# One DiT layer on one core: another order of the first loads, and an FFN stage with folded columns, gate rows in two passes and features that go by DRAM

## The chip, the cores and the metric

The kernel runs on one core of a Trainium2 chip, and its metric is the device time of one execution in microseconds (us). The core's engines are PE (matmul; its weight loads are shown apart as PEld), DVE (vector), ACT (scalar), POOL (GpSimd) and SP, which here only issues DMAs. Each engine works through its own list in order. DMAs that SP and ACT issue stand in two queues.

## The reference, cut to what is computed

```python
sh1, sc1, g1, sh2, sc2, g2 = split(silu(c) @ w_ada + b_ada, 6)        # ada: 2048 -> 6 x 2048
u  = x * (1 + sc1) + sh1                                              # 256 latent tokens
uc = ctx * (1 + csc1) + csh1                                          # 256 context tokens, their own ada row
q, k, v = u @ w_in, uc @ w_in                                         # 2048 -> 3072; 16 heads of 128, 4 kv heads
heads = [window attention with sinks (8 heads), global attention with normed q, k (8 heads)]
x = layer_norm(ALPHA * x + g1 * (heads @ w_out)) * ln1_g + ln1_b
z = x * (1 + sc2) + sh2
x = layer_norm(ALPHA * x + g2 * ((silu(z @ w_gate) * (z @ w_up)) @ w_down)) * ln2_g + ln2_b   # 2048 -> 5632 -> 2048
```

All inputs and the output are float32.

## The kernel before

**Products.** Every large product is made of three: each operand is split into a high part, rounded to the type f32r (ACT casts it), and a low part, the rest (DVE subtracts it). `mm3` (lines 277 to 280) then issues x_high·w_high, x_high·w_low and x_low·w_high into one PSUM bank, a row tile of 128 tokens against 512 columns. A matmul in plain float32 stands twice in the trace, in f32r once.

**Weights** come in tiles of 1 MB (`load_raw`, L248, on SP's queue) into 4 buffers of the pool `raw`, and are split in two halves (`split_raw`: ACT `hi` L268, DVE `lo` L269) into 4 pairs of buffers `hi`, `lo`. A weight tile is 24 matmuls of the FFN stage: 4 slices of 128 features, 2 row tiles, 3 products.

**First part, up to about 404 us.** A planner (class `Flow`) gets steps with costs, dependences, earliest times (`since`) and buffers, and writes the instructions of all engines in the order that it finds. It holds the ada vector for layer norm 1's inputs, the q/k/v product in five groups of features (`GROUPS`), attention, and the output product. The context and the latent `u` need ada columns: PE multiplies `cs` (silu of c) with w_ada (L570), or DVE does it with weighted sums (`vector_sum`, `csum`, `adav`, `g1b`). `WARM` small matmuls against the identity (L1237) are steps of the planner that keep PE at work where it has nothing; `EARLY_WARM` of them (L322) stand ahead of the first transposition. The planner's list for PE starts with its free time in the table at line 460.

**The start.** ACT issues the DMAs of `c` and `c_ctx` (crow), waits for PE to transpose them, takes silu, and only then issues the first 128 columns of x and ctx and the ada bias `brow` (L333 to L336). PE transposes `brow` at L466 and x at L738.

**FFN stage, first half** (`first_half`, from 404 to about 590 us). Gate and up of the first ten of eleven column blocks f are made in two halves. For f < `ONE_F` the first half takes only the features 0 to 511, else 0 to 1023 (`groups`); the sums go to buffers `spills`. Meanwhile (`merge` interleaves lists evenly) the features 512 to 2047 of z are made ready: DVE sums w_ada rows over 16 steps into `adav`, a row on each partition (`ada_vector_steps`, L393); `second_columns_of` turns them into columns, 8 float32 matmuls against `ones` (L1099), or 4 in `second_scales` (L1395); POOL makes the scale mA and shift mB (`combine`, L1092 to L1094); `z_part` transposes two slices of the normed x on PE (L1434), applies scale and shift on ACT (L1438) and splits (L1440, L1441) into `u2h`, `u2l`, on which the later matmuls work.

```python
    run(merge(first_half[3 : 2 * ONE_F], scales))
    combine(1)
    z_part(4)
    z_part(6)
    cutoff = len(first_half) - 2
    run(merge(first_half[2 * ONE_F : cutoff], side))
    for kk in range(EARLY_G * 4, KD, 2):
        z_part(kk)
    run(first_half[cutoff:])
```

Here `side` is the sums and columns of the feature groups 2 and 3. Outside the planner's part the framework's scheduler sets the order of the instructions on each engine.

**Second half and down product.** The other features follow; hidden features reach their transposed layout by DVE block transposes (`squares`), DMAs to DRAM (`put`, 4 per row tile) and back (`get`), without PE. Beside the down product, DVE sums the rows of the gate g2, and a float32 matmul against `ones` (`rows_from`, L403) spreads each of four pieces of 512 over the partitions.

Of the kernel before, what the change touches and what calls it, by code (L numbers as in the profile page):

```python
# [22 lines left out]
P = 128  # L23
D = 2048
# [24 lines left out]
EARLY_WARM = 2  # L49
COLD = 7  # L50
# [3 lines left out]
ONE_F = 3  # L54
# [149 lines left out]
def dit_layer(ctx: ExitStack, tc: tile.TileContext, x, c, cx, c_ctx, w_ada, b_ada, w_in, q_norm_g,  # L204
# [114 lines left out]
    nc.scalar.dma_start(crow[KD : 2 * KD, :], c_ctx.rearrange("(k p) -> k p", p=P))  # L319
    early = wk_bank()  # L320
# [11 lines left out]
    first_cx = xt[:, :, D - P :]  # L332
    nc.scalar.dma_start(xt[:, :, :P], x[:, :P].rearrange("(t p) d -> p t d", p=P))  # L333
    nc.scalar.dma_start(first_cx, cx[:, :P].rearrange("(t p) d -> p t d", p=P))
    brow = pa.tile([6 * KD, P], F32, tag="brow", name="brow")
    nc.scalar.dma_start(brow, b_ada.rearrange("o (n p) -> (o n) p", p=P))  # L336
# [6 lines left out]
    ones = main.tile([P, P], F32, tag="ones", name="ones")  # L343
    nc.gpsimd.memset(ones, 1.0)
# [54 lines left out]

    def rows_from(sb, dst, s):  # L400
# [36 lines left out]
    def const_tables():  # L437
        nc.gpsimd.tensor_scalar_mul(nsink, sinkb, -1.0)
        for t in range(NT):
            for g, cg, sg in ((gq, cosQ, sinQ), (gk, cosK, sinK)):  # L440
# [19 lines left out]
             {"SP": 1300.0, "PE": 3500.0, "ACT": 5000.0, "DVE": 4000.0, "POOL": 4000.0})  # L460
# [43 lines left out]
    def flow_weights(w, k0, nk, c0, width=NB, where=("raw", "araw"), spare=False):  # L504

        raw, ld = flow_load(w, k0, nk, c0, width, where)
        pieces = []
        for s in range(0, nk * width, SUB * NB):
            n = min(SUB * NB, nk * width - s)
            hl = Buf("b4" if spare else "hl")  # L510
            hl.rooms = [hl, Buf("b4")] if spare else [hl]

            def cast(hl=hl, s=s, n=n):
                if spare:
                    hl.hi, hl.lo = (b4([P, SUB * NB], F32R, c) for c in ("hi", "lo"))
                else:
# [7 lines left out]
            a = F.add("ACT", 60 + 0.87 * n, cast, [ld], hl.rooms)  # L524
# [32 lines left out]
    def flow_columns(c0, ncol, shift, scale, ats, at):  # L557
# [253 lines left out]
    def flow_blocks(g, bs, where=("raw", "araw")):  # L811

        k0, n = GROUPS[g]
        if n == 1:
            for i, (b0, m) in enumerate(((2, 1), (0, 2), (3, 2), (5, 1))):
                F.at = bs[0] + (bs[1] - bs[0]) * i / 4
                piece, = flow_weights(w_in, k0, 1, b0 * NB, m * NB, ("b4",))
# [284 lines left out]

    def second_place(g, ps):
# [288 lines left out]
    def second_scales(sb):  # L1392
        ps = wk_bank()
        for j in range(4):
            nc.tensor.matmul(ps[:, 2 * j : 2 * j + 2], lhsT=sb[:, j * P : (j + 1) * P], rhs=ones[:, 0:2], start=True, stop=True)  # L1395
        nc.vector.tensor_scalar_add(sc2[:, 4:8, :], ps[:, 0:8].rearrange("p (j s) -> p j s", s=2), 1.0)
# [33 lines left out]
    def z_part(kk):  # L1430
        ps = wk_bank()
        for j in range(2):
            for t in range(NT):
                nc.tensor.transpose(ps[:, (j * 2 + t) * P : (j * 2 + t + 1) * P],  # L1434
                                    xt[:, t, (kk + j) * P : (kk + j + 1) * P], ident)
        uf = pb.tile([P, 2, SEQ], F32, tag="t2k", name="uf2", bufs=4)
        for j in range(2):
            nc.scalar.activation(uf[:, j, :], ps[:, j * SEQ : (j + 1) * SEQ], AF.Identity,  # L1438
                                 bias=mB[:, kk + j : kk + j + 1], scale=mA[:, kk + j : kk + j + 1])
        nc.scalar.copy(u2h[:, kk : kk + 2, :], uf)  # L1440
        nc.vector.tensor_tensor(u2l[:, kk : kk + 2, :], uf, u2h[:, kk : kk + 2, :].bitcast(F32), op=ALU.subtract)  # L1441
# [102 lines left out]
    scales = ada_vector_steps((4 * D + NB,), NB, lambda: late_sums[1]()[:, :NB], second_scales)  # L1544
# [25 lines left out]
    scalars(1)  # L1570
    adav1 = vector_sums(NB)
# [160 lines left out]
```

## Time and profile before

| | |
|---|---|
| time, median of 3 runs | 1138.57 us (1138.26 to 1139.23) |
| time of the profiled execution | 1141.69 us, of which its span is 1139.9 |
| PE busy | 1116.1 us, 98% of the span, 5287 instructions |
| DVE, ACT, POOL busy | 859.9 us (75%), 564.2 us (49%), 42.0 us (4%) |
| DMA | 321.26 MB, mean 282 GB/s |
| shares of the chain that ended last | PE 85%, DVE 7%, DMA 5%, issue 1%, ACT 1% |

The span is the profiled stretch of one execution; its time is 1.8 us more, and 3.1 us above the median of the runs. The chain is followed back from the last instruction to whatever released each step. A busy PE is not a PE at its peak, since the ends of matmuls are modelled: how fast it goes is seen in the distance of their starts.

### The profile page before, as it was taken

How to read it: one execution, taken by the hardware profiler on the slowest of the kernel's cores; microseconds unless marked ns; L12 is line 12 of the kernel's file. 1: busy time of each engine (PE TensorE's matmuls, PEld its weight loads, DVE VectorE, ACT ScalarE, POOL GpSimd, SP SyncE). 2: the span in 40 equal slices, each digit the busy share in tenths (PEclk: the TensorE clock that was granted, in tenths of full speed). 3: DMA queues.
4: the chain of work that ended last, by engine and by line, in shares of the span. 5: the costliest groups of instructions: out<-in, count | busy, mean ns of one | idle time of the engine just before them, and what ended most of it. 6: DMA issues, size and time to landing. Idle time of an engine off the chain costs nothing.

```text
span 1139.9 us, 14170 instructions
## 1 busy us (share of the span) xinstructions
PE 1116.1 (98%) x5287; PEld 903.9 (79%) x5287; DVE 859.9 (75%) x1074; ACT 564.2 (49%) x815; POOL 42.0 (4%) x82
## 2 busy tenths in 40 slices
PE   7999999999999999999999999999999999999995
PEld 6766778787888788888888888888888888888884
DVE  3758999999998897767767566776766787676556
ACT  2435574877785265444464444445444344333441
POOL 1000040101200000010000000000000000000000
PEclk9999999999999999999999999999999999999998
DMA  9999999788999689989866776777676989877531
GB/s 299 353 363 394 399 338 371 250 277 251 340 333 398 230 315 324 320 310 316 304 217 222 236 238 223 231 246 257 218 251 238 314 314 332 317 273 264 193 134 74
DMA packets 186413, 321.26 MB, mean 282 GB/s; under 512 B 8764, under 2 KB 51164, under 8 KB 184039
## 3 DMA queue, kind: packets, MB, share of 16 engines
q1 hardware_dynamic: 184536, 319.25, 80.7%
q10 hardware_dynamic: 1808, 1.11, 0.3%
q8 instruction: 41, 0.67, 0.2%
q14 instruction: 28, 0.23, 0.1%
HBM read 304.07 MB, written 16.25 MB: 281 GB/s over the span
## 4 chain that ended last, share of the span: by engine, by line
PE 85%; DVE 7%; DMA 5%; issue 1%; ACT 1%; SPq 0%; DVEq 0%; ACTq 0%
PE acc L278 26%; PE acc L280 25%; PE acc L279 25%; DMA raw<-in_w_ada_dram 3%; PE wk L1046 2%; DVE csum L634 2%; DMA raw<-in_w_in_dram 2%; DVE g1b L393 2%; PE wk L570 1%; DVE lo L522 1%; DMA brow<-in_b_ada_dram 1%; PE wk L278 1%; PE wk L280 1%; PE wk L279 1%; PE wk L403 1%
## 5 line engine op out<-in xcount | busy, mean ns | idle before, releaser
L269 DVE TENSOR_TENSOR lo<-raw,hi 128x1024 fp32r<-128x1024 f32 x258 | 312.5, 1221 | 179.7 <-ACT hi L268 176.3
L268 ACT CAST hi<-raw 128x1024 fp32r<-128x1024 f32 x258 | 271.0, 1055 | 343.8 <-PE acc L280 296.8
L278 PE MATMUL acc<-hi,u2h 128*128 128x512 f32 x704 | 274.6, 390 | 0.0
L280 PE MATMUL acc<-hi,u2l 128*128 128x512 f32 x704 | 274.1, 389 | 0.0
L279 PE MATMUL acc<-lo,u2h 128*128 128x512 f32 x704 | 274.0, 389 | 0.0
L280 PEld LDWEIGHTS acc<-hi,u2l 128*128 128x128 f32 x704 | 132.1, 188 | 27.9 <-DVE u2l L1556 0.5
L278 PEld LDWEIGHTS acc<-hi,u2h 128*128 128x128 f32 x704 | 132.2, 188 | 27.9 <-ACT u2h L1555 0.8
L279 PEld LDWEIGHTS acc<-lo,u2h 128*128 128x128 f32 x704 | 132.2, 188 | 27.8 <-DVE lo L269 0.4
L278 PE MATMUL acc<-hi,hTh 128*128 128x512 f32 x344 | 135.5, 394 | 0.0
L280 PE MATMUL acc<-hi,hTl 128*128 128x512 f32 x344 | 133.9, 389 | 0.0
L279 PE MATMUL acc<-lo,hTh 128*128 128x512 f32 x344 | 133.9, 389 | 0.0
L519 ACT CAST hi<-raw 128x1024 fp32r<-128x1024 f32 (+1 forms) x86 | 87.7, 1032 | 93.0 <-PE acc L280 54.0
L393 DVE SCALAR_TENSOR_TENSOR adav<-raw,cs,adav 128x512 f32<-128x512 f32 (+1 forms) x128 | 121.2, 947 | 12.6 <-DMA raw<-in_w_ada_dram 10.9
L522 DVE TENSOR_TENSOR lo<-raw,hi 128x1024 fp32r<-128x1024 f32 (+1 forms) x86 | 101.7, 1196 | 22.7 <-ACT hi L519 22.6
L278 PE MATMUL acc<-hi,uh 128*128 128x512 f32 x256 | 103.4, 404 | 0.8 <-ACT acc L534 0.8
L279 PE MATMUL acc<-lo,uh 128*128 128x512 f32 x256 | 100.3, 392 | 1.5 <-DVE lo L522 1.5
L280 PE MATMUL acc<-hi,ul 128*128 128x512 f32 x256 | 100.1, 391 | 0.1
L278 PEld LDWEIGHTS acc<-hi,hTh 128*128 128x128 f32 x344 | 64.6, 188 | 14.4 <-issue 1.0
L279 PEld LDWEIGHTS acc<-lo,hTh 128*128 128x128 f32 x344 | 64.6, 188 | 14.3 <-issue 1.0
L280 PEld LDWEIGHTS acc<-hi,hTl 128*128 128x128 f32 x344 | 64.6, 188 | 13.3
L278 PEld LDWEIGHTS acc<-hi,uh 128*128 128x128 f32 x256 | 48.2, 188 | 17.7 <-issue 5.0
L279 PEld LDWEIGHTS acc<-lo,uh 128*128 128x128 f32 x256 | 48.2, 188 | 11.5 <-DVE lo L522 2.6
(216 smaller groups left out, 1195.7 us busy)
## 6 DMA issues: line engine op xcount, KB each, us to landing
raw<-in_w_ada_dram SPq DMA_DIRECT2D x63, 1024.0 KB, 7.5
raw<-in_w_gate_dram SPq DMA_DIRECT2D x44, 1024.0 KB, 6.2
raw<-in_w_up_dram SPq DMA_DIRECT2D x44, 1024.0 KB, 5.3
raw<-in_w_down_dram SPq DMA_DIRECT2D x44, 1024.0 KB, 5.0
raw<-in_w_ada_dram SPq DMA_DIRECT2D x66, 512.0 KB, 6.4
raw<-in_w_in_dram SPq DMA_DIRECT2D x18, 1024.0 KB, 7.9
raw<-in_w_out_dram SPq DMA_DIRECT2D x16, 1024.0 KB
pd<-hx SPq DMA_DIRECT2D x64, 128.0 KB, 3.9
```

What stands on the lines that cost most here:

```text
L268: nc.scalar.copy(hi[:, :n], raw[:, s : s + n])
L269: nc.vector.tensor_tensor(lo[:, :n], raw[:, s : s + n], hi[:, :n].bitcast(F32), op=ALU.subtract)
L278: nc.tensor.matmul(ps, lhsT=xh, rhs=w[0], start=first, stop=False, skip_group_check=seeded)
L279: nc.tensor.matmul(ps, lhsT=xh, rhs=w[1], start=False, stop=False, skip_group_check=seeded)
L280: nc.tensor.matmul(ps, lhsT=xl, rhs=w[0], start=False, stop=last, skip_group_check=seeded)
L393: nc.vector.scalar_tensor_tensor(a[:, c : c + piece], raw[:, f : f + piece], cs[:, 4 * (g * (G4 * NB // w) + j) + 2, None], a[:, c : c + p ...
L403: nc.tensor.matmul(ps, lhsT=ones, rhs=sb[:, s : s + NB], start=True, stop=True)
L519: nc.scalar.copy(hl.hi[:, :n], raw.t[:, s : s + n])
L522: nc.vector.tensor_tensor(hl.lo[:, :n], raw.t[:, s : s + n], hl.hi[:, :n].bitcast(F32), op=ALU.subtract)
L570: nc.tensor.matmul(bank.t[32 * j : 32 * j + 32, :width], lhsT=cs[:, 4 * k + 2 - 2 * i : 4 * k + 34 - 2 * i], rhs=raw.t[:, c * width : (c + ...
L634: nc.vector.scalar_tensor_tensor(a, src, cs[:, k, None], a, op0=ALU.mult, op1=ALU.add)
L1046: nc.tensor.matmul(o_ps.t[:, : 2 * P].rearrange("p (g q) -> p g q", q=32), lhsT=v, rhs=pv[:, k], start=k == 0, stop=k == 3)
```

## The change

1. **Start.** ACT issues `brow`, x and ctx right behind `c` and `c_ctx`, ahead of its wait for PE. `EARLY_WARM` goes from 2 to 5; of the 56 planned warm-ups 3 in place of 7 are costed as cold; PE's list starts at 5600 in place of 3500; three `since` times are set. With other times the planner finds another order for the whole first part.
2. **Columns.** `columns_by_squares` replaces the float32 matmuls against `ones` for the groups 1 to 3: per 512 columns a DVE block transpose and a DVE sum over 32, then the 4 small matmuls of `fold_parts`, which the first part has already (L685).
3. **Normed features.** The 24 PE transposes of `z_part` go. DVE makes block transposes of the normed x into unused `spills` (`z_squares`), SP's queue carries them to DRAM (`z_puts`) and back (`z_gets`) into the place of `u2h`, and `z_place` applies scale and shift from there. Puts and gets are steps merged into the FFN stage, the puts behind 2 empty steps.
4. **Gate rows.** Each piece is split in two f32r parts (ACT, DVE), and two f32r matmuls replace the float32 one.
5. `ONE_F` 3 to 4: block f = 3 takes only the features 0 to 511 in the first half. `ones` is written by ACT, no longer by POOL.

```diff
-EARLY_WARM = 2
-COLD = 7
+EARLY_WARM = 5
+COLD = 3
...
-ONE_F = 3
+ONE_F = 4
...
+    brow = pa.tile([6 * KD, P], F32, tag="brow", name="brow")
+    nc.scalar.dma_start(brow, b_ada.rearrange("o (n p) -> (o n) p", p=P))
+    first_cx = xt[:, :, D - P :]
+    nc.scalar.dma_start(xt[:, :, :P], x[:, :P].rearrange("(t p) d -> p t d", p=P))
+    nc.scalar.dma_start(first_cx, cx[:, :P].rearrange("(t p) d -> p t d", p=P))
     early = wk_bank()
...
+    def add_rows(ps, pair):
+        nc.tensor.matmul(ps, lhsT=ones_r, rhs=pair[0], start=True, stop=False)
+        nc.tensor.matmul(ps, lhsT=ones_r, rhs=pair[1], start=False, stop=True)
...
-                rows_from(sb, dst, s)()
+                pair = [pb.tile([P, NB], F32R, tag="t2k", name="rowpair", bufs=4) for _ in range(2)]
+                split_rows(pair, sb[:, s : s + NB])
+                ps = wk_bank()
+                add_rows(ps, pair)
+                nc.scalar.copy(dst[:, s : s + NB], ps)
...
+    def columns_by_squares(sb, n):
+
+        ps = wk_bank()
+        part = pb.tile([P, 1, n * 4], F32, tag="part", name="part", bufs=2)
+        for s in range(0, n * P, NB):
+            turned = pb.tile([P, NB], F32, tag="t2k", name="turned", bufs=4)
+            nc.vector.transpose(turned, sb[:, s : s + NB])
+            nc.vector.reduce_sum(part[:, 0, s // 32 : (s + NB) // 32], turned.rearrange("p (b j) -> p b j", j=32), axis=AX.X)
+        fold_parts(ps, part, n)
+        return ps[:, :n, None]
...
-            second_place(g, second_columns_of(sb))
+            place_columns(g, columns_by_squares(sb, 8))
             combine(g)
...
+    def z_squares(n, t):
+        squares(xt[:, t, n * NB : (n + 1) * NB], spills[SPLIT_F - n][0][:, t, :])
+
+    def z_puts(n):
+        zd[n] = [put(spills[SPLIT_F - n][0][:, t, :]) for t in range(NT)]
...
+            for j in range(2):
+                k = 4 * n + q + j
+                nc.scalar.activation(uf[:, j, :].rearrange("p (t a i) -> p t a i", t=NT, a=4), hv[:, q + j], AF.Identity,
+                                     bias=mB[:, k : k + 1], scale=mA[:, k : k + 1])
+            ufs.append(uf)
+        for uf, k in zip(ufs, (4 * n, 4 * n + 2)):
+            nc.scalar.copy(u2h[:, k : k + 2, :], uf)
+            nc.vector.tensor_tensor(u2l[:, k : k + 2, :], uf, u2h[:, k : k + 2, :].bitcast(F32), op=ALU.subtract)
...
-    run(merge(first_half[3 : 2 * ONE_F], scales))
+    z_puts(1)
+    run(merge(first_half[3 : 2 * ONE_F], scales, [nothing, lambda: z_gets(1), nothing]))
     combine(1)
-    z_part(4)
-    z_part(6)
+    z_place(1)
...
-    for kk in range(EARLY_G * 4, KD, 2):
-        z_part(kk)
+    run(merge(first_half[2 * ONE_F : cutoff], side, sum(([nothing] * 2 + m for m in moves), []) + [nothing] * 12))
+    for n in range(EARLY_G, ng):
+        z_place(n)
     run(first_half[cutoff:])
```

On PE, at the very start, these rows stood ahead of the q/k/v products (before; L324 transposes crow, L570 is ada on PE, L1237 a warm-up):

```order
L324 MATMUL wk<-ident,crow 128x32
L1237 MATMUL wk<-ident 128x128 x14
L570 MATMUL wk<-raw,cs 32x128 x16
L466 MATMUL wk<-ident,brow 128x96
L1237 MATMUL wk<-ident 128x128
L738 MATMUL wk<-ident,xt 128x128 x2
L570 MATMUL wk<-raw_155,cs 32x128 x8
```

The same place after the change:

```order
L329 MATMUL wk<-ident,crow 128x32
L1266 MATMUL wk<-ident 128x128 x5
L583 MATMUL wk<-raw,cs 32x128 x16
L1266 MATMUL wk<-ident 128x128 x3
L479 MATMUL wk<-ident,brow 128x96
L1266 MATMUL wk<-ident 128x128 x2
L751 MATMUL wk<-ident,xt 128x128 x2
L583 MATMUL wk<-raw_153,cs 32x128 x8
```

Nine of the 14 warm-ups ahead of the first ada product are gone from there, and five stand around the transposition of `brow`. Behind these rows both orders go on alike up to the first product: 2 transposes, 4 warm-ups, 8 ada matmuls, 3 warm-ups, L604 (now L617), 11 warm-ups.

On ACT, where the features 1024 to 2047 get scale and shift, ahead of the last tiles of the first half (before; `hi` is a weight half's cast, `uf2` a scaled slice, its source `wk` a PSUM bank):

```order
L268 CAST hi_5205<-raw_5203 128x1024
L268 CAST hi_5209<-raw_5203 128x1024
L268 CAST hi_5239<-raw_5237 128x1024
L1540 COPY spill_3786<-acc_5070 128x512
L1540 COPY spill_3786<-acc_5071 128x512
L1438 ACTIVATE uf2_5166<-wk_5161,mB_141,mA_140 128x256 x2
L1438 ACTIVATE uf2_5176<-wk_5171,mB_141,mA_140 128x256
```

and after, where hi_5163 is the first cast of the tile behind it (the counterpart of hi_5205):

```order
L268 CAST hi_5109<-raw_5103 128x1024
L1476 ACTIVATE uf2_5139<-u2h_3767,mB_144,mA_143 128x256 x2
L1476 ACTIVATE uf2_5142<-u2h_3767,mB_144,mA_143 128x256 x2
L1476 ACTIVATE uf2_5149<-u2h_3767,mB_144,mA_143 128x256
L1480 CAST u2h_3767<-uf2_5139 128x512
L1480 CAST u2h_3767<-uf2_5142 128x512
L1476 ACTIVATE uf2_5149<-u2h_3767,mB_144,mA_143 128x256
L1476 ACTIVATE uf2_5152<-u2h_3767,mB_144,mA_143 128x256 x2
L268 CAST hi_5163<-raw_5161 128x1024
```

The scaling stood behind three weight casts that are needed later; now it stands ahead of the next one. The slices uf2_5149 and uf2_5152 are of group 3, whose mA and mB come from the last columns.

On PE the last columns stand here after the change (L698 is `fold_parts`):

```order
L278 MATMUL acc_5045<-hi_5105,u2h_3767 128x512
L278 MATMUL acc_5046<-hi_5105,u2h_3767 128x512
L698 MATMUL wk_5086<-part_5087,fold_108 32x8 x4
L279 MATMUL acc_5045<-lo_5106,u2h_3767 128x512
L280 MATMUL acc_5045<-hi_5105,u2l_3768 128x512
...
L280 MATMUL acc_5046<-hi_5109,u2l_3768 128x512
L278 MATMUL acc_5159<-hi_5163,u2h_3767 128x512
L278 MATMUL acc_5160<-hi_5163,u2h_3767 128x512
L279 MATMUL acc_5159<-lo_5164,u2h_3767 128x512
```

Between the fold and the first use of hi_5163 there are 22 matmuls of that tile; before, the columns (L1099) stood ahead of the counterpart of acc_5045<-hi_5105, and the 16 transposes right ahead of the counterpart of hi_5163's first use.

## Rows read from the trace of the kernel before

**Rows 1.** Windows by stage: length, busy times, PE's clock, DMA share, GB/s.

```profile
core 0: us, PE busy (x) PEld busy (x) DVE busy (x) ACT busy (x) POOL busy (x), PEclk, DMA share, GB/s
0.00:22.60 22.60, 15.45 (x143) 13.76 (x143) 5.68 (x10) 5.63 (x11) 3.48 (x9) 0.92 0.98 287
22.60:48.00 25.40, 25.40 (x206) 20.15 (x209) 19.82 (x32) 10.33 (x18) 0.00 (x0) 1.00 1.06 364
48.00:78.00 30.00, 30.00 (x190) 18.95 (x183) 18.17 (x27) 8.64 (x13) 0.00 (x0) 1.00 0.96 340
78.00:146.00 68.00, 65.54 (x354) 48.44 (x353) 60.00 (x60) 38.88 (x62) 0.00 (x0) 1.00 1.05 395
146.00:205.00 59.00, 58.70 (x276) 47.66 (x274) 56.68 (x66) 35.45 (x60) 13.85 (x16) 1.00 0.95 352
205.00:386.00 181.00, 180.42 (x815) 145.49 (x816) 171.07 (x291) 127.54 (x263) 14.03 (x38) 1.00 0.90 305
...
438.00:580.00 142.00, 142.00 (x652) 118.30 (x651) 101.29 (x90) 68.81 (x82) 5.24 (x7) 1.00 0.88 307
580.00:1118.60 538.60, 538.60 (x2370) 444.52 (x2369) 366.98 (x403) 237.79 (x256) 1.58 (x3) 1.00 0.72 245
```

**Rows 2.** Chain of waits in the first 24 us: start, length, what.

```profile
0.74 5.82 DMA raw<-in_w_ada_dram
...
6.58 7.86 DMA brow<-in_b_ada_dram
...
15.31 0.81 PE wk L570 x16
...
20.24 2.56 PE wk L1237 x22
```

**Rows 3.** Waits of SP's queue from 22 to 80 us.

```profile
SPq L496 <- PE wk L570: 24.0, 10, 6.3
```

**Rows 4.** Chain of waits at five places of the FFN stage.

```profile
430.18 0.79 PE wk L1395 x8
430.97 0.93 PE wk L1434 x8
...
437.59 0.50 PE acc L279
...
570.08 1.68 PE wk L1099 x16
571.76 0.35 PE acc L278
...
577.37 1.75 PE wk L1434 x16
...
910.99 0.86 PE wk L403 x2
```

**Rows 5.** Timeline of PE at the first part's one fold.

```profile
149.54 0.26 PE L685 MATMUL wk<-cpart,fold 128*32 128x16 f32 x8
149.73 0.49 PE L278 MATMUL acc<-hi,uh 128*128 128x512 f32 x1
150.07 0.43 PE L279 MATMUL acc<-lo,uh 128*128 128x512 f32 x1
```

**Rows 6.** Timeline of POOL, then of ACT, from 572 to 584 us.

```profile
572.12 1.11 POOL L1092 TENSOR_TENSOR mA<-lcol,sc 128x4 f32<-128x4 f32 x1 [69.00 <-DVE sc L1107]
...
573.46 0.20 POOL L1094 TENSOR_TENSOR mB<-mB,sh 128x4 f32<-128x4 f32 x1
...
577.90 1.48 ACT L1438 ACTIVATE uf<-wk,mB,mA 128x256 f32<-128x256 f32 x3
579.27 0.62 ACT L1440 CAST u2h<-uf 128x512 fp32r<-128x512 f32 x1
...
583.08 1.07 ACT L268 CAST hi<-raw 128x1024 fp32r<-128x1024 f32 x1
```

**Rows 7.** Source line of DVE's block transposes: ns min, median, max.

```profile
L1479 DVE STREAM_TRANSPOSE spill<-spill x20: 667/686/705, 624.6 to 842.9; 128x512 f32<-128x512 f32 x20
```

More of the change, by code (lines that the diff above doesn't have):

```diff
@@ L331, in dit_layer @@
     )
[L332 to L336, printed above, removed]
     sel = main.tile([P, 4], F32, tag="sel", name="sel")
@@ L342, in dit_layer @@
     nc.vector.reduce_sum(fold, ident.rearrange("p (a i) -> p i a", a=4), axis=AX.X)
-    ones = main.tile([P, P], F32, tag="ones", name="ones")
-    nc.gpsimd.memset(ones, 1.0)
+    ones_r = main.tile([P, P], F32R, tag="ones", name="ones")
+    nc.scalar.activation(ones_r, ident, AF.Copy, bias=1.0, scale=0.0)
+    ones = ones_r.bitcast(F32)
     bcol = main.tile([P, 6 * KD], F32, tag="bcol", name="bcol")
@@ L459, in dit_layer @@
     F = Flow({"raw": RAW_BUFS, "araw": ADA_BUFS, "hl": HL_BUFS, "acc": 4, "wk": 4, "b4": NB4, "t2k": T2K},
-             {"SP": 1300.0, "PE": 3500.0, "ACT": 5000.0, "DVE": 4000.0, "POOL": 4000.0})
+             {"SP": 1300.0, "PE": 5600.0, "ACT": 5000.0, "DVE": 4000.0, "POOL": 4000.0})
     pools = {"raw": wraw, "araw": araw}
@@ L522, in rest @@
                 nc.vector.tensor_tensor(hl.lo[:, :n], raw.t[:, s : s + n], hl.hi[:, :n].bitcast(F32), op=ALU.subtract)
-            a = F.add("ACT", 60 + 0.87 * n, cast, [ld], hl.rooms)
+            a = F.add("ACT", 60 + 0.87 * n, cast, [ld], hl.rooms, since=since)
             b = F.add("DVE", 60 + 1.06 * n, rest, [a], give=[raw])
@@ L816, in flow_blocks @@
                 F.at = bs[0] + (bs[1] - bs[0]) * i / 4
-                piece, = flow_weights(w_in, k0, 1, b0 * NB, m * NB, ("b4",))
+                piece, = flow_weights(w_in, k0, 1, b0 * NB, m * NB, ("b4",), since=14000.0 if i and g == 0 else 0.0)
                 for j in range(m):
@@ L1392, in second_scales @@
     def second_scales(sb):
[L1393 to L1396, printed above, removed]
+        nc.vector.tensor_scalar_add(sc2[:, 4:8, 0:1], columns_by_squares(sb, 4), 1.0)
     def scalars(t):
@@ L1428, in dit_layer, with z_home, z_gets, z_place @@
     hTl = [pb.tile([P, 4, SEQ], F32R, tag=f"hTl{f}", name="hTl") if f < KF // 4 - SPLIT_F else None for f in range(KF // 4)]
[L1430 to L1441, printed above, removed]
+    def z_squares(n, t):
+        squares(xt[:, t, n * NB : (n + 1) * NB], spills[SPLIT_F - n][0][:, t, :])
+    def z_puts(n):
+        zd[n] = [put(spills[SPLIT_F - n][0][:, t, :]) for t in range(NT)]
+    def z_home(n):
+        return u2h[:, 4 * n : 4 * n + 4, :].bitcast(F32).rearrange("p q s -> p (q s)").rearrange("p (t x) -> p t x", t=NT)
+    def z_gets(n):
+        for t in range(NT):
+            get(zd[n][t], z_home(n)[:, t, :])
+    def z_place(n):
+        hv = z_home(n).rearrange("p t (a q i) -> p q t a i", a=4, q=4)
+        ufs = []
+        for q in range(0, 4, 2):
+            uf = pb.tile([P, 2, SEQ], F32, tag="t2k", name="uf2", bufs=4)
+            for j in range(2):
[6 more added lines that the diff above has]
+            nc.vector.tensor_tensor(u2l[:, k : k + 2, :], uf, u2h[:, k : k + 2, :].bitcast(F32), op=ALU.subtract)
+    zd = {}
     def residual_base(n):
@@ L1570, in dit_layer @@
     scalars(1)
+    for t in range(NT):
+        normalise(1, t)
+        z_squares(1, t)
     adav1 = vector_sums(NB)
@@ L1585, in dit_layer, with later, nothing @@
             nc.scalar.copy(spills[0][i][:, t, :], firsts[i][t])
-    for n in range(1, 4):
-        for t in range(NT):
-            normalise(n, t)
+    nc.vector.memset(scale_sums[:, :2], 0.0)
     region.__exit__(None, None, None)
+    def later(n, t):
+        normalise(n, t)
+        z_squares(n, t)
+    def nothing():
+        pass
     run(first_half[2:3])
-    run(merge(first_half[3 : 2 * ONE_F], scales))
+    z_puts(1)
+    run(merge(first_half[3 : 2 * ONE_F], scales, [nothing, lambda: z_gets(1), nothing]))
     combine(1)
-    z_part(4)
-    z_part(6)
+    z_place(1)
     cutoff = len(first_half) - 2
-    run(merge(first_half[2 * ONE_F : cutoff], side))
-    for kk in range(EARLY_G * 4, KD, 2):
-        z_part(kk)
+    moves = [[lambda n=n, t=t: later(n, t) for n in range(EARLY_G, ng) for t in range(NT)],
+             [lambda n=n: z_puts(n) for n in range(EARLY_G, ng)], [lambda n=n: z_gets(n) for n in range(EARLY_G, ng)]]
+    run(merge(first_half[2 * ONE_F : cutoff], side, sum(([nothing] * 2 + m for m in moves), []) + [nothing] * 12))
+    for n in range(EARLY_G, ng):
+        z_place(n)
     run(first_half[cutoff:])
```

14 lines of the change are left out of this document (11 added, 3 removed).

## Prediction

> **What bounds the kernel now.** I read the windows by stage first, because the mean of 98% hides where PE had room. From 438 us on PE is busy for every us of every window: 142.00 of 142 and 538.60 of 538.60, at the full clock of 1.00 (2.4 GHz) [rows 1]. What PE doesn't have to do there comes off the end, one for one, as long as nothing else is late. DVE (101.29 of 142) and the DMA engines (share 0.88) have room.
>
> Before 205 us two bounds run side by side. PE is hardly idle from 22.6 us on, yet the DMA engines are full too: shares of 1.06, 0.96 and 1.05 [rows 1]. From 78 to 146 us they move 395 GB/s and PE is idle for 2.5 us of 68; from 48 to 78 us they move only 340, and SP's queue spends 24.0 us waiting until PE has used an ada tile and so frees a buffer [rows 1, 3]. So PE holds back the loads up to 78 us, and the loads hold back PE after that.
>
> The chain of waits shows the start: the first ada load lands at 6.56 us, the chain then goes to `brow`, issued at 6.58 and landed at 14.44, and to 22 records (11 matmuls) of warm-up up to 22.80, where the first q/k/v product stands [rows 2]. PE's list had `brow` in the way.
>
> **The terms, part by part.** Minus is faster.
>
> *Columns and transposes.* The chain shows, at 430.18, 0.79 us of columns and 0.93 of transposes; at 570.08, 1.68 of columns, and a next matmul of 0.35 in place of its usual 0.23; at 577.37, 1.75 of transposes [rows 4]. Group 2 repeats the columns once more, about 73 us earlier, with the same two numbers. Removed: 1.72 + 2 x (1.68 + 0.12) + 1.75 = 7.07. Also the matmul at 437.59 took 0.50, which is 0.27 of waiting for the split of the new features [rows 4]; one weight tile more now stands between, so I count it as gone. Added: three folds. The one in the first part starts at 149.54, the next matmul at 149.73, and the one after that 0.34 later in place of 0.23 [rows 5]: 0.30 each, 0.9. Net -6.2, and the 0.3 of waiting.
>
> *Gate rows.* A float32 spread stands for 0.86 us [rows 4], four times; two f32r matmuls take 0.23 each, the pace of the second half (538.60 us for 2370 [rows 1]): 4 x (0.86 - 0.46) = -1.6. The two more split steps per piece lie on ACT and DVE, which have 301 and 172 us of idle time between 580 and 1118.6 us [rows 1]. If that cover failed, a piece would cost a cast, 0.62, and a DVE pass, 0.69 at most [rows 6, 7].
>
> *What is late instead: z_place.* The scaling of groups 2 and 3 now stands on ACT ahead of the next weight tile's cast, hi_5163, and its second half needs mA and mB of the last columns. Counted from the start of the last fold: the fold 0.25; from the end of the old columns (571.76) until POOL is through with mB (573.46 + 0.20) 1.90 us [rows 4, 6]; then ACT does four slices and two casts. Three slices took 1.37 us from start to start, a cast 0.51 to the next one, so 4 x 0.46 + 2 x 0.51 = 2.86; the weight cast takes 1.07 [rows 6]. It ends at 6.1. PE is there after the fold and 22 matmuls of 0.23, at 5.3. So it waits 0.8; then two matmuls of 0.23, and the low half (DVE, some 1.2 behind the cast, as twice the columns of a 0.69 pass [rows 7]) is 0.7 late; the next half's, behind two spills and two casts on ACT, 0.4. Together +1.9. Lower bound 0, if the scheduler's order leaves more cover than I count; upper bound 3.7, if all three of POOL's steps take 1.11 as the first did [rows 6]. I take 1.9, as POOL was like this at this place.
>
> *The row tile 1 of group 0.* Five of the six new block transposes, 0.69 us each [rows 7], and three normalisations stand on DVE ahead of this tile's splits, where three sums stood. PE needs these splits around 403 us. DVE has small gaps there. +0.9, between 0 and 3.4 (five transposes).
>
> *Puts and gets.* 24 puts and 6 gets stand on SP's queue between weight loads, 3 MB of traffic to and fro. They lie beside PE's products; behind them on the queue are weight and ada loads, and for those PE waits only when the cushion of split tiles is used up. Since `ONE_F` = 4 leaves 22 weight tiles in place of 26 for the same 16 tiles of ada sums, this stretch asks for (22 + 16) x 1.05 + 2 = 42 MB in 22 x 24 x 0.227 = 120 us, 350 GB/s, where it moved 307 [rows 1]. The saturated stretch moved 395 [rows 1]. So 0; the upper bound is the stretch at 340, as from 48 to 78 us: 42 MB then take 123.5, +3.5.
>
> *Start.* `brow`, x and ctx come 4 to 5 us earlier. The first ada load then lands later, since 0.3 MB more goes out with it; at 287 GB/s that is 1.1 us, so about 7.7. From there PE has 16 ada matmuls, 4 warm-ups and then the same rows that took 8.36 us from 14.44 to 22.80 [rows 2]; 8 ada matmuls took 0.81 at most, and a warm-up 0.23. 7.7 + 1.6 + 0.9 + 8.36 = 18.6 at the old pace. The granted clock has a mean of 0.92 in this window [rows 1], so 0.08 x 22.6 = 1.8 us of work at 2.4 GHz were lost to a stretch at 1.2; without the long wait for `brow` ahead of it I take the clock as full, 16.8. PE gets a lead of 4.2 to 6.0 us.
>
> How much of it lasts? The loads cannot start earlier; they can only lose their holes. From 48 to 78 us they fall short of 395 GB/s by 55, which is 30 x 55 / 395 = 4.2 us of loading; from 22.6 to 48 by 31, 2.0 us [rows 1]. An earlier PE frees buffers earlier and fills these. After 78 us the loads set the pace. I take -3.5: most of the first hole, since the rows of the second are partly short ones that are slow anyway. Bounds 0 and -6.0.
>
> On this start, the Trainium skill (DMA: Bandwidth & Descriptors, Issuing engines are not separate DMA queues) says that transfers of all issuing engines run on the same 16 DMA engines and interleave, so that an issue moved on ACT's queue brings no bandwidth. The trace agrees: the share is 0.98 with both queues at work in the first window. By that rule taken alone the start would bring nothing, which is the second case below.
>
> *Order of the first part.* The planner has reordered neighbours on PE and SP up to 386 us; number and size of the steps are the same. 0, between -2.5 (PE's idle time from 78 to 146 us [rows 1]) and the loss in the fourth case.
>
> **Sum.** -6.2 - 0.3 - 1.6 + 1.9 + 0.9 - 3.5 = -8.8. The profiled execution took 1141.69, so 1132.9; it was 3.1 above the median of the runs, which gives 1129.8 for a median.
>
> **The rivals.**
> 1. As summed: **1129.8**, with its own bounds from 1127 to 1132.
> 2. The lead at the start is lost, because the loads are full from 2 us on. For it: the shares above 1. Against it: SP's 24.0 us of waiting for PE. 1138.6 - 5.3 = **1133.3**.
> 3. The whole lead lasts, and the scheduler's cover makes z_place and the splits free: 1138.6 - 6.2 - 0.3 - 1.6 - 6.0 = **1124.5**.
> 4. On the other side: the new order of the first part makes DVE wait. DVE is busy for 227.75 of the 240 us from 146 to 386 [rows 1], and PE hangs on it. If its 12.2 us of idle time there double, the end moves by as much: 1138.6 - 8.8 + 12.2 = **1142.0**. The change is slower from 8.8 us on. Against it: only neighbours are swapped.
> 5. The folds wait: the columns are ready only after two transposes and two sums over 32 on DVE, each at most 0.69 [rows 7], where PE's old columns followed the last ada sum at once. If none of it is hidden, 2.8 + 2.8 + 1.4 = 7.0 comes back: **1136.8**. Against it: DVE was idle for 41 us of the 142 [rows 1].
>
> **How the numbers follow.** Chances: case 1 0.52, case 2 0.20, case 3 0.10, case 4 0.09, case 5 0.09. The predicted time is that of case 1. A range from 1125.5 to 1134.5 takes in cases 1 and 2 with their spread and some of case 3, and leaves out 0.2. A difference under 0.2% (2.3 us) can't be told from none here. Cases 1 to 3 and most of 5 are faster by more: 0.89; the rest of 5 and a little of 4 are the same: 0.05; most of 4 is slower: 0.06.
>
> **What the profile after would show.** No transposes of xt on PE behind 404 us; three folds of about 0.3 us, each without a wait for DVE; four pairs of f32r matmuls of 0.46. PE waiting once, near 570 us, on ACT's cast and DVE's low half, 2 us in all. The first q/k/v product near 16 to 18 us, more than 340 GB/s from 40 to 75 us, and SP's waits for L583 well below 24. The prediction is wrong if PE's busy windows after 404 us have holes at the gets, if the first product comes early and the attention's end (386 us before) doesn't move, or if DVE's idle time from 140 to 380 us grows.

## The result, and the profile after

The changed kernel took **1142.62 us** (median of 20 runs, 1138.76 to 1144.87) beside 1139.43 us before (20 runs, 1138.19 to 1142.72). The ratio, taken over all runs, is 1.0021 (that of the two medians is 1.0028), 95% interval 1.0013 to 1.0029: it became slightly slower, where 1129.8 was forecast. The profiled execution took 1143.72 us. Of the 20 runs, the five with a mean granted clock of 0.995 or 0.996 took 1138.76 to 1140.99 us, and the fifteen with 0.991 to 0.994 took 1141.48 to 1144.87.

Windows by stage of the changed kernel, with the columns of [rows 1]:

```profile
0.00:22.60 22.60, 19.54 (x167) 17.22 (x168) 8.12 (x17) 7.92 (x15) 3.34 (x8) 1.00 1.01 288
22.60:48.00 25.40, 22.64 (x200) 17.09 (x202) 15.68 (x25) 8.32 (x14) 0.00 (x0) 0.93 1.07 371
48.00:78.00 30.00, 30.00 (x178) 19.34 (x171) 18.69 (x29) 9.38 (x13) 0.00 (x0) 1.00 1.03 378
78.00:146.00 68.00, 67.92 (x364) 51.04 (x362) 62.14 (x60) 39.91 (x64) 0.00 (x0) 1.00 1.04 380
146.00:205.00 59.00, 58.52 (x276) 47.59 (x276) 55.07 (x66) 36.13 (x60) 13.81 (x16) 1.00 0.96 355
205.00:386.00 181.00, 180.24 (x824) 145.77 (x823) 169.19 (x290) 126.20 (x260) 13.06 (x41) 1.00 0.89 302
386.00:404.00 18.00, 15.58 (x89) 9.61 (x88) 17.61 (x40) 6.21 (x16) 1.44 (x2) 1.00 0.75 252
...
438.00:580.00 142.00, 135.64 (x596) 109.03 (x594) 106.02 (x101) 69.49 (x89) 3.57 (x7) 0.99 0.89 314
580.00:1118.60 538.60, 538.52 (x2375) 445.39 (x2374) 369.48 (x405) 237.81 (x253) 1.58 (x3) 1.00 0.74 248
```

Three windows have lost PE time: 22.6 to 48, 386 to 404, and above all 438 to 580 us, where PE was busy for all 142 us before and has 6.4 us of holes now. To see what each is worth I counted PE's products in both traces, which do the same ones, and compared the start of the n-th of a kind (after minus before):

```
                        before     after    difference
q/k/v product    1       22.56     16.65      -5.90
                49       39.34     38.79      -0.54
               385      149.73    146.56      -3.17
output product 384      390.65    387.57      -3.08
FFN product     97      419.14    418.66      -0.48
               193      442.94    440.82      -2.12
               673      553.60    558.14      +4.55
               769      578.87    582.49      +3.62
down product     1      883.62    887.13      +3.51
              1032     1123.64   1126.02      +2.38
```

So 3.1 us are won up to attention's end, 2.6 of them are lost at once, 1.6 come back at the columns of group 1, 6.7 are lost between 441 and 558 us, and 2.2 come back behind that. PE's waits there by what it waited for (us in total, times, longest):

```profile
PE acc L278 <- ACT hi L268: 4.1, 3, 1.6
PE acc L279 <- DVE lo L269: 2.3, 4, 0.7
PE acc L280 <- DVE u2l L1599: 1.9, 1, 1.9
PE wk L1433 <- DVE xt L1201: 0.5, 1, 0.5
```

PE waits for the cast of a weight tile, twice for 1.6 us, up to 486.12 and 511.78, and once for 0.8, up to 570.43. From start to start the products on either side of the first two stand 2.01 us apart in place of 0.23, so I call each a hole of 1.78 us; two products later PE waits again, for the low half, and comes 0.69 late. The chain of waits shows the second:

```profile
510.68 1.06 ACT hi L268
511.76 1.24 DVE lo L269
513.04 0.50 PE acc L279
...
513.88 0.43 PE acc L279
```

Behind this hole the products come 0.43 us apart in place of 0.23. The windows say why: the granted clock has a mean of 0.72, so part of the time is at 1.2 GHz, after PE stood idle for 1.6 and 0.5 us. By my estimate that costs 0.28 x 6 = 1.7 us more. It does not follow every hole: behind that at 486, which is as long, the clock stays at 1.00.

```profile
486.00:490.00 4.00, 3.36 (x13) 2.47 (x14) 3.87 (x4) 3.01 (x4) 0.00 (x0) 1.00 1.03 339
508.00:512.00 4.00, 2.38 (x11) 1.69 (x10) 0.24 (x1) 2.39 (x4) 0.00 (x0) 1.00 1.00 367
512.00:518.00 6.00, 5.47 (x17) 3.98 (x17) 5.96 (x6) 2.56 (x3) 0.00 (x0) 0.72 0.48 142
```

My first suspect was SP's queue. Its timeline shows the puts (L1526) of the groups 2 and 3 as two bursts of eight, in which no weight is issued for 7.81 and 6.85 us:

```profile
460.43 7.81 SPq L1526 DMA_DIRECT2D hd<-spill  x8
468.34 0.39 SPq L248 DMA_DIRECT2D raw<-in_w_up_dram  x1
468.83 0.97 SPq L384 DMA_DIRECT2D raw<-in_w_ada_dram  x2
469.85 6.85 SPq L1526 DMA_DIRECT2D hd<-spill  x8
476.80 0.39 SPq L248 DMA_DIRECT2D raw<-in_w_gate_dram  x1
```

### The profile page after: what moved, and what is told of

Read it like the earlier page. It is cut to its first block, busy times and chain, and to the rows that moved or that the text cites. A ratio compares the mean times of both kernels' runs of the same rounds, so it can differ in the third digit from the quotient of the medians.

```text
span 1141.9 us, 14178 instructions
## 1 busy us (share of the span) xinstructions
PE 1113.1 (97%) x5253; PEld 898.4 (79%) x5253; DVE 868.9 (76%) x1095; ACT 566.1 (50%) x820; POOL 38.3 (3%) x81
## 4 chain that ended last, share of the span: by engine, by line
PE 80%; DVE 9%; DMA 6%; issue 2%; ACT 1%; SPq 1%; POOL 0%; DVEq 0%; ACTq 0%
PE acc L279 24%; PE acc L280 24%; PE acc L278 24%; DMA raw<-in_w_ada_dram 5%; PE wk L1059 2%; PE wk L583 2%; DVE g1b L394 1%; DMA raw<-in_w_in_dram 1%; DVE adav L394 1%; DVE lo L535 1%; SPq L509 1%; DVE csum L647 1%; DVE lo L269 1%; PE wk L278 1%; PE wk L280 1%
## 5 line engine op out<-in xcount | busy, mean ns | idle before, releaser
L280 PEld LDWEIGHTS acc<-hi,ul 128*128 128x128 f32 x256 | 48.5, 189 | 11.0 <-DVE ul L767 0.4
```

The costliest lines, as they stand in the source:

```text
L280: nc.tensor.matmul(ps, lhsT=xl, rhs=w[0], start=False, stop=last, skip_group_check=seeded)
```

## The experiments

Sixteen kernels, each timed against the kernel before on the same chip.

**x1, ONE_F back at 3.**

```diff
-ONE_F = 4
+ONE_F = 3
```

> The changed kernel with ONE_F back at 3; all else as changed. In the changed kernel the products of the stretch from 480 to 530 us come out 6.4 us later against before than they stood at 479 us, in holes behind late weight tiles. Theory A (the puts of the features hold up the weight loads): the holes stay, about as large, and the time is 1141 to 1143 us. Theory B (ONE_F = 4 asks for 350 GB/s, since 22 weight tiles now cover the same 16 tiles of ada sums): with 26 tiles the holes go, and the time is 1136 to 1138 us.

1144.48 us, ratio 1.0037 (1.0025 to 1.0050). The holes of 1.78 us stand at 489.7 and 515.4, at a lower demand. The demand is not the cause.

**x2, the features transposed by PE as before.** `z_part` comes back in place of squares, puts, gets and `z_place`:

```diff
-    z_puts(1)
...
-    z_place(1)
+    z_part(4)
+    z_part(6)
```

> The changed kernel with the features of groups 1 to 3 transposed by PE as before (no block transposes, puts and gets of them, and their normalisations back in their old place); ONE_F stays 4, columns, gate rows and start stay changed. Theory A (puts): the holes of 480 to 530 us go (7.9 us with what the columns should have saved there), also the 2.6 us of waiting at 394 to 399 us and the 2.3 us at 570 us; the transposes and the wait behind them bring back 2.95 us: 1142.6 - 12.8 + 2.95 = 1132.8 us. Theory B (ONE_F): only the waits at 394 and 570 us go: 1140.7 us.

1134.90 us, ratio 0.9959 (0.9946 to 0.9971). From 438 to 580 us PE is busy for 142.00 us again, and of the waits from 386 to 580 us one is left:

```profile
PE acc L280 <- DVE u2l L1612: 1.2, 1, 1.2
```

So the features by DRAM cost all that the rest wins, and more. They don't answer for the wait at 394 us alone: 1.2 of its 1.9 us stay.

**x3, puts issued by ACT.**

```diff
-            nc.sync.dma_start(hd[:, :, a, :]...
+            q.dma_start(hd[:, :, a, :]...        # q = nc.scalar for the features
```

> The changed kernel with the puts of the features (24 DMAs of 64 KB) issued by ACT instead of SP. Theory A1 (SP's queue is what the puts hold up: 8 of them took 7.8 us there, the next 8 took 6.9 us, and no weight load is issued meanwhile): the holes shrink by most of their 6 us, 1136 to 1138 us. Theory A2 (the puts' small packets fill the DMA engines: 716 and 845 bytes on average and 192 and 257 GB/s where 390 were moved): the holes stay, 1141 to 1144 us.

1139.25 us, ratio 0.9998 (0.9989 to 1.0007). The holes at 486 to 512 us are gone, a new one of 2.1 us stands at 443. The time lies between the two that were expected. It speaks for A1, but ACT's puts came at other times too (399 to 443 us), so it didn't settle it.

**x4, x11 and x16: the start alone, the earlier loads alone, the planner's numbers alone,** each on the kernel before.

```diff
-EARLY_WARM = 2          # x4, x16: with COLD, PE's 5600 and the three times
+EARLY_WARM = 5
...
+    nc.scalar.dma_start(brow, ...)      # x4, x11: with x and ctx, ahead of the wait for PE
```

> The kernel before with the start of the change alone (order of the first loads, EARLY_WARM, COLD, PE's 5600, the three times). Theory: the lead of 3.1 us that the changed kernel has at the end of attention's output product lasts to the end, since PE waits for nothing behind it: 1139.4 - 3.1 = 1136.3 us. Rival: the lead is given up later, because the loads from 404 to 580 us set the pace: 1139 us, with PE waiting for weights there.

> The kernel before with the earlier issue of brow, x and ctx alone; EARLY_WARM, COLD, PE's 3500 and the times are as before, and so is the planner's order. The whole start part gave 1137.5 beside 1139.6 us. If the earlier loads are what helps: 1137.5. If it is the planner's other order of the first part: 1139.6.

> The kernel before with the planner's numbers of the start part alone (EARLY_WARM 5, COLD 3, PE's 5600, the three times), brow, x and ctx issued as before. The whole start part gave -2.1 us, the earlier issue alone +0.1. If the other order of the first part brings the gain: 1137.5 to 1138 us. If it needs both: 1139.6 us or more.

x4: 1137.52 us, ratio 0.9988 (0.9976 to 1.0001). x11: 1140.19, 1.0002 (0.9993 to 1.0010). x16: 1139.35, 1.0000 (0.9988 to 1.0012). If the start part has a gain, it needs both halves, and the interval of x4 just reaches none.

**x5, the folded columns alone, and x6, the gate rows alone,** on the kernel before.

```diff
-            second_place(g, second_columns_of(sb))                  # x5
+            place_columns(g, columns_by_squares(sb, 8))
...
-                rows_from(sb, dst, s)()                              # x6
...
+                add_rows(ps, pair)
```

> The kernel before with the folded columns alone (part 2 of the change); features by PE, gate rows, start and ONE_F as before. By the terms of the prediction: 0.79 + 2 x 1.80 us of old columns go, three folds of 0.30 us come, so -3.5 us: 1136.1 us beside 1139.6. Rival (the prediction's fifth case): the folds wait on DVE's two transposes and two sums, and the time is 1138 us or more.

> The kernel before with the gate rows in two f32r passes alone (part 4). The prediction's term is -1.6 us (1138.0 beside 1139.6); the changed kernel's products show 1.1 us won over the four pieces, three pieces of 0.36 and one of nothing (1138.5). Rival: the two more split steps on ACT and DVE hold up weights, and nothing is left (1139.6).

x5: 1137.17 us, ratio 0.9981 (0.9973 to 0.9990); in its trace the groups 2 and 3 win 1.4 us each, group 1 loses 0.4, since PE now comes 1.03 us late at 438 us for the split features. The folds don't wait for DVE there. x6: 1139.46 us, ratio 0.9993 (0.9984 to 1.0002), which can't be told from none; in its trace the down product gets 1.14 us shorter.

**x7, x2 with ONE_F = 3** (the edits of x1 and x2 together).

> The changed kernel with the features of groups 1 to 3 transposed by PE as before, and ONE_F back at 3, so that of the five parts only start, columns and gate rows are left. If ONE_F does nothing by itself: as the run with PE's transposes and ONE_F = 4, 1134.9 us, within 0.7. If ONE_F = 4 has a cost that the smaller traffic of that run hid: 1133 to 1134 us. If it has a gain: 1136 us.

1135.60 us, ratio 0.9968 (0.9956 to 0.9980), within the spread of x2: no effect of ONE_F is seen. The three parts alone give 0.0012 + 0.0019 + 0.0007 = 0.0038, together 0.0032: they add up within their intervals of some 0.001 each. Part 3 then costs 1.0021 - 0.9968 = 0.0053, 6 us.

**x8, groups 2 and 3 by DRAM with ACT's puts and a later scaling, group 1 by PE.**

```diff
-    for n in range(EARLY_G, ng):
-        z_place(n)
+    z_place(2)
     run(first_half[cutoff:])
+    z_place(3)
```

> Start, columns, gate rows and ONE_F = 4 as changed; group 1 of the features by PE's transposes; groups 2 and 3 by DRAM, but with the puts issued by ACT and with the scaling put behind the last weight tiles of the first half, where nothing needs it for another tile. If the cost of the features by DRAM was only in SP's queue and in the place of the scaling: the run with PE's transposes (1134.9 us) less the 1.75 us of transposes at the end of the first half: 1133.1 us. If their traffic or their issues cost something wherever they stand: 1135 us or more.

1134.26 us, ratio 0.9949 (0.9937 to 0.9961). From the 193rd FFN product on it wins 1.5 us over x2, where 1.75 were expected; up to the 97th it loses 2.3 more, where the framework's scheduler put block transposes ahead of the split.

**x9, puts spread, and x12, one DMA per put.**

```diff
-             [lambda n=n: z_puts(n) for n in range(EARLY_G, ng)]
+             [lambda: z_put(2, 0), nothing, lambda: z_put(2, 1), nothing, lambda: z_put(3, 0), nothing, lambda: z_put(3, 1)], ...
```

In x12, where the gets become four DMAs each in return:

```diff
-        zd[n] = [put(spills[SPLIT_F - n][0][:, t, :]) for t in range(NT)]
...
+            nc.sync.dma_start(hd.rearrange("a i r x -> (a i) (r x)"), spills[SPLIT_F - n][0][:, t, :])
```

> The changed kernel with the puts of groups 2 and 3 spread over four places of SP's queue, 4 DMAs at each, with weight and ada loads in between, in place of 8 and 8 within 17 us. Same DMAs, same queue, same bytes; the gets come a few loads later. If it is the burst on SP's queue that makes the weights late: SP is held for 2 to 3 us at a time, which the split weights in store cover, the holes of 480 to 530 us go or shrink to 2 us, and the time is 1135 to 1137 us. If the small packets or the bytes as such are what the stretch can't carry: the holes stay, at other places, 1141 to 1143 us.

> The changed kernel with each put of the features as one DMA of whole rows (2 KB packets) in place of four with 512 byte packets; the order is made by the gets instead, four DMAs with 512 byte reads per row tile in place of one. Number of DMAs and bytes are the same. If the small packets written from 460 to 478 us, and SP's wait behind them, make the holes: these go, and the gets, which stand between other loads, make smaller ones at 490 to 510 us: 1137 to 1140 us. If small packets cost the same wherever they are: 1142 to 1144 us.

x9: 1143.38 us, ratio 1.0028 (1.0016 to 1.0039). x12: 1143.87 us, ratio 1.0028 (1.0019 to 1.0038). In x9 four puts hold SP for 1.9 to 2.7 us:

```profile
460.43 1.92 SPq L1530 DMA_DIRECT2D hd<-spill  x4
...
492.52 2.72 SPq L1530 DMA_DIRECT2D hd<-spill  x4
```

and the hole of 1.78 us at 509.5 stays, with another of 1.1 at 535. In x12, where 16 gets hold SP for 10.47 us, holes of 1.1 to 1.5 us stand at 485, 505 and 514. My theory of the burst fell, and that of the small packets written too. I looked at the holes again: in the changed kernel, x1, x9 and x10, whatever came late, the largest had the same size, and ACT's timeline of the changed kernel shows what they have in common (idle time before an instruction and what ended it in brackets):

```profile
472.98 1.27 ACT L1582 COPY spill<-acc 128x512 f32<-128x512 f32 x2 [2.96 <-PE acc L280]
474.14 2.00 ACT L268 CAST hi<-raw 128x1024 fp32r<-128x1024 f32 x2
483.86 1.26 ACT L1582 COPY spill<-acc 128x512 f32<-128x512 f32 x2 [7.72 <-PE acc L280]
485.02 1.99 ACT L268 CAST hi<-raw 128x1024 fp32r<-128x1024 f32 x2
```

ACT stands for 7.72 us in front of the copies of a block, because PE has not finished it. The next tile's cast is behind them in ACT's list. That tile, issued at 476.80, landed 5.3 us later, at 482.1, so it lay there for 1.8 us before ACT came to the copies. PE ends the block at 484.34, the copies take 1.16 us from start to start, the cast 1.1, and PE goes on at 486.12. In x2 ACT's list has a cast of the next tile ahead of the copies, and PE meets no hole:

```profile
481.30 1.05 ACT L268 CAST hi<-raw 128x1024 fp32r<-128x1024 f32 x1 [1.67 <-PE acc L280]
483.34 1.27 ACT L1595 COPY spill<-acc 128x512 f32<-128x512 f32 x2 [0.98 <-PE acc L280]
484.50 1.05 ACT L268 CAST hi<-raw 128x1024 fp32r<-128x1024 f32 x1
```

It can be read from the order of ACT's list without a run. A block is two tiles, four casts; between the copies of one block and the next the list of the changed kernel has

```
L1582 COPY spill<-acc 128x512 x2
L268 CAST hi<-raw 128x1024 x4
L1582 COPY spill<-acc 128x512 x2
L268 CAST hi<-raw 128x1024 x2
L1582 COPY spill<-acc 128x512 x2
L268 CAST hi<-raw 128x1024 x5
L1582 COPY spill<-acc 128x512 x2
L268 CAST hi<-raw 128x1024 x3
L1582 COPY spill<-acc 128x512 x2
```

ACT's lead is two casts; where only two stand between copies, it falls to none: the hole at 486. Five bring it to one, three to none: the hole at 512. In x2 there are three to five, and the lead stays above none. The wait of 0.70 at 499 is another one: there DVE's low half stands behind its transposes and sums for the columns of group 2.

**x10, the scaling of groups 2 and 3 later** (the edit of x8 on the changed kernel).

> The changed kernel with the scaling of groups 2 and 3 one and two weight tiles later (ahead of and behind the last two tiles of the first half). If the wait at 570 us is there because the weight cast stands behind the scaling on ACT, and the scaling behind POOL: the 1.7 us of holes and 0.6 us of slow matmuls behind them go, 1140.3 us beside 1142.6. Rival: the wait only moves to the first tile that needs the features: 1142 us or more. The holes of 480 to 530 us stay in both.

1140.75 us, ratio 1.0005 (0.9996 to 1.0014). The wait at 570 us is gone, the others stay.

**x13, ACT's order fixed.** The copies stand behind the casts of the next tile, and ACT keeps the written order:

```diff
         w = load_split(w_, g * 4, f * NB)
+        while waiting:
+            nc.scalar.copy(*waiting.pop(0))
...
-                        nc.scalar.copy(spills[f][i][:, t, :], st["accs"][t])
+                        waiting.append((spills[f][i][:, t, :], st["accs"][t]))
...
+    with tc.manual_schedule(engines={ET.Activation}):
+        run(merge(first_half[2 * ONE_F : cutoff], side, ...
```

> The changed kernel with ACT's order in the first half of the FFN stage fixed: each block's two copies into the spill buffers stand behind the casts of the next block's first tile, never ahead of them. SP's order of puts, gets and loads there is the same. Theory D (ACT's order makes the holes): those at 486, 499 and 512 us go, with the slow matmuls behind them, 7.9 us in all; the wait at 570 us stays: 1142.6 - 7.9 = 1134.7 us. Theory C (the weight tiles land too late behind the puts): PE waits for them all the same, the holes get smaller by the copies' 1.2 us each but stay: 1139 to 1141 us.

1135.68 us, ratio 0.9967 (0.9955 to 0.9980): 6 us, with the same puts in the same places of SP's list. ACT's timeline:

```profile
475.69 2.00 ACT L268 CAST hi<-raw 128x1024 fp32r<-128x1024 f32 x2
483.70 2.00 ACT L268 CAST hi<-raw 128x1024 fp32r<-128x1024 f32 x2 [6.01 <-DMA raw<-in_w_gate_dram]
485.61 1.06 ACT L1501 COPY spill<-acc 128x512 f32<-128x512 f32 x2
```

The weight tile is late, ACT waits 6.01 us for it; but it casts when the tile lands, ahead of the end of PE's block, and PE goes on. So a tile that lands late makes no hole by itself here; the order does. From the 193rd to the 673rd FFN product x13 takes 110.48 us, the changed kernel 117.32, the kernel before 110.66. By the forecast of the columns 1.3 us are still lost, and the trace has 1.1 of them at 498 us: PE's fold waits for DVE's sums, 0.23 us, and the next product for a low half behind them, 0.88. DVE's last ada sum ends at 495.1 there, in x2 at 488.0; I did not test whether the puts ahead of the ada loads do this.

**x14, x13 with the later scaling, and x15, x8 with ACT's order fixed** (no edit but those of x10, x8 and x13).

> As the run with ACT's order fixed, and the scaling of groups 2 and 3 one and two tiles later. By theory D and the run with the later scaling alone (2.3 us at 570 us): 1134.7 - 2.3 = 1132.4 us, the whole change without its two order faults. If the scaling now meets the copies: 1134 to 1135 us.

> The best version so far (group 1 by PE, groups 2 and 3 by DRAM with ACT's puts and the later scaling, 1134.3 us) with ACT's order fixed in the same way. It had no holes from 440 to 580 us, so theory D gives nothing: 1134.3 us within 0.7. If fixing the order has a price of its own (ACT waits for a load with copies ready): 1135 us or more.

x14: 1134.60 us, ratio 0.9951 (0.9938 to 0.9964). x15: 1143.26 us, ratio 1.0022 (1.0009 to 1.0034). In x15 the puts stand on ACT in written order:

```profile
472.30 1.27 ACT L1514 COPY spill<-acc 128x512 f32<-128x512 f32 x2 [3.70 <-PE acc L280]
472.99 5.90 ACTq L1543 DMA_DIRECT2D hd<-spill  x8
478.99 1.04 ACT L268 CAST hi<-raw 128x1024 fp32r<-128x1024 f32 x1 [5.42 <-DMA hd<-spill]
```

Eight puts hold ACT itself for 5.9 us, and the casts with it. In x3 and x8 the scheduler had put them earlier (399 to 443 us and 394 to 421 us) and in smaller groups; in x8 a cast waits 2.73 us behind one, but PE has no hole from it.

## Why the prediction was wrong, by its own steps

**The step that failed is "Puts and gets", counted as 0** with an upper bound of 3.5. I asked whether the DMA engines could carry the bytes, and took PE's split tiles as a cushion, but did not look at what sets that cushion: the place of the block copies in ACT's list, which the framework's scheduler had changed. From 441 to 558 us the forecast was -1.5 (group 2's columns) and the trace shows +6.7: 8.2 us off. By x13 some 6 to 7 us of this are ACT's order. The whole forecast was 11.2 us off (-8.8 for +2.4 by the ratio); some 2.1 of the rest are the start, 0.5 each row tile 1 and the gate rows. None of my rivals was this one; the fourth, on the slow side, is refuted: DVE's idle time from 146 to 386 us did grow, to 15.7 us from 12.2, which I had named as a sign against me, but attention ends 3.1 us early. The fifth shows in small, in the wait of 0.70 at 499 us.

Why the scheduler chose this order is not shown. What is: with the puts on SP it did so in five versions (the changed kernel, x1, x10, x12, and x9 with three casts twice in place of two), without them or with them on ACT not at this place.

**The bandwidth bound** asked for 350 GB/s over the stretch. It moved 314 from 438 to 580 us, and in x1, at a lower demand, the holes were the same. That sum answered a question that did not decide.

**z_place, +1.9:** right. Its row of the chain reads

```profile
566.84 1.13 ACT u2h L1480 x2
567.96 1.49 ACT uf L1476 x3
569.45 0.94 ACT hi L268
570.41 1.24 DVE lo L269
571.69 0.50 PE acc L279
```

PE's products come 1.0 and 0.7 us late, for 0.8 and 0.7 forecast; the third wait, 0.4, did not come, and the clock stayed at 1.00 from 572 to 576 us. The path is the forecast one: from the fold's start at 564.20 over POOL to the end of the cast it took 6.2 us, for 6.1. x10 took away 0.0016 (1.0021 - 1.0005), 1.8 us.

**Columns and transposes, -6.2 and -0.3:** the columns were right for groups 2 and 3 (-1.4 each in x5 for -1.50), and the fold stands as counted, here that of group 1:

```profile
435.07 0.25 PE L698 MATMUL wk<-part,fold 128*32 128x4 f32 x8
```

In the changed kernel the wait of 437.59 [rows 4] is gone as forecast; from product 97 to 193 it won 1.64 for 1.69. In x5, with PE's transposes kept, that wait grew.

**Gate rows, -1.6:** measured -1.13. Two matmuls take 0.23 each in the chain, as said:

```profile
914.50 0.24 PE wk L406
914.74 0.24 PE wk L407
```

From the start of a piece to the second product behind it, less one product's 0.23, it is 0.86 before and 0.46 to 0.49 now: the 0.40 of the forecast, or little less, four times. What is missing are 0.35 us that PE loses anew at 954 us, where its weight load waits for DVE's low half:

```profile
PEld acc L279 <- DVE lo L269: 0.5, 1, 0.5
```

(The expectation of x6 took this for a piece that wins nothing.)

**Row tile 1 of group 0, +0.9:** 2.6 us were lost there (1.9 and 0.5 of waiting). x2 without the block transposes, and x4 with the start alone, lose 1.2 and 1.5 at the same place. So the transposes cost 1.4, near the forecast. The rest comes with the planner's other order: x16, with its numbers alone, loses 1.2 there too, and x11, with the earlier loads alone, nothing. DVE, at 17.61 of 18 us, could not follow.

**Start, -3.5:** x4 gave 0.0012, 1.4 us (2.1 by the medians), and of the 3.1 at attention's end 1.2 are that loss at 394 us. The first product came at 16.65 us, in the forecast 16 to 18, but the 49th only 0.54 us early:

```profile
17.96 8.68 DMA raw<-in_w_in_dram
26.73 0.62 ACT hi L532
27.34 0.50 ACT qacc L816
27.88 0.50 PE acc L278
```

The product at 27.88 is the 31st. Its weights, like those of all the first 48, were split by 20.2 us; what it waits for, 2.8 us, is a PSUM bank, which ACT's copy of a finished sum to `qacc` frees. In ACT's list this copy stands behind the cast of the tile for the 49th product, and ACT waits 6.95 us for that tile's load, which landed at 26.64:

```profile
16.16 2.64 ACT L532 CAST hi<-raw 128x1024 fp32r<-128x1024 f32 x3
...
26.73 0.62 ACT L532 CAST hi<-raw 128x512 fp32r<-128x512 f32 x1 [6.95 <-DMA raw<-in_w_in_dram]
```

So this wait, too, is ACT's order, here a copy behind a cast. The planner's other order made it: x16 has the cast first as well, while in the kernel before, x5 and x11 the copy stands first, and in x5 the 48 products go through without a wait. PE then ran at a mean granted clock of 0.60 for 4 us, as the second window shows:

```profile
24.00:28.00 4.00, 1.25 (x6) 0.70 (x6) 0.63 (x2) 1.10 (x2) 0.00 (x0) 1.00 1.05 366
28.00:32.00 4.00, 4.00 (x12) 3.08 (x13) 3.13 (x5) 2.12 (x3) 0.00 (x0) 0.60 1.10 351
```

That the lead is lost up to 48 us is what the second case said, but not by its reason: it is a load that lands no earlier together with a list that makes PE wait for it. Whether the loads behind it would have let PE keep the lead is not shown. What came later did so as I had said: 378 GB/s from 48 to 78 us in place of 340, and PE busy for 67.92 of 68 us from 78 on. SP's wait for PE is 21.7 us beside 24.0 [rows 3], not well below it:

```profile
SPq L509 <- PE wk L583: 21.7, 11, 5.7
```

**The baseline.** The profile of before had a slow start: x5 and x6, whose start is the same, show their first product at 20.79 and 20.21 us and the 49th at 37.53 and 36.98, where it stood at 22.56 and 39.34 (the 22.80 that I took for the first product is the end of the warm-ups). Part of what I wanted to win at the start was that one execution's.

## What to carry to other kernels

Where a change adds work beside a stage that one engine bounds, don't stop at bytes and busy shares: compare the order of the lists of the engines that feed it, and count how far each runs ahead at every instruction that waits for the bound engine. A copy out of a finished block, placed ahead of the next block's first cast, cost 2.5 us each time, and once a slow clock on top, though ACT was busy half the time; at the start a copy behind a cast that waits for its load cost PE 2.8 us.

A gain from a start is worth what is left of it behind the next load that PE, by whatever way, waits for; it should be read from several executions, not from one.

## What the runs showed of the hardware that was not expected

The start differs from one execution to the next, and so does the clock behind its wait. In the six profiles with the first q/k/v product at 16.45 to 16.99 us the 49th stands at 38.60 to 39.19; in nine with 18.3 to 20.8 us, five of them with the new start, it stands at 36.57 to 37.93. The load lands at 26.6 to 26.8 us in either kind (the chains of the changed kernel, x2 and x4). But it is not the early product that is dear. In x9 and x13, with the first product at 17.36 and 17.24 us, PE waits 2.2 us as well, the granted clock stays at 1.00, and the 49th stands at 37.37 and 37.22. In the six PE waits 2.3 to 3.1 us and the clock has a mean of 0.57 to 0.67 from 28 to 32 us; the row of x13 is

```profile
28.00:32.00 4.00, 4.00 (x31) 3.12 (x35) 3.48 (x6) 2.61 (x4) 0.00 (x0) 1.00 1.11 355
```

So the loss of 1.2 to 2 us goes with the slow clock behind the wait. The holes at 486 and 512 us agree: they are alike, and the clock fell behind one of them. What decides it is not shown.

Issuing a burst of 64 KB stores is not cheap beside full DMA engines (share 0.92 from 460 to 480 us): eight puts held SP for 7.81 us and, in x15, ACT for 5.90 us, 0.7 to 1.0 us each; four in x9 took 1.92 us, 0.5 each. In the burst of 7.81 us the first five also stand 0.5 us apart, and the last begins 3.35 us after the one ahead of it (464.59 and 467.94). The Trainium skill (DMA: Bandwidth & Descriptors, Issuing engines are not separate DMA queues) says that issuing from a second engine saves only the time to initiate a DMA, usually small beside the DMA itself. A single put of the changed kernel agrees, with a median of 0.43 us for the issue and 4.7 us to landing; a burst does not, and its time is what the queue's owner loses.
